# The first gate unit's first half between the two halves of keys and values, and the second half's keys from normalised operands

## The chip, the cores and the metric

The kernel runs on one core of one Trainium2 chip. The metric is device time of one execution in microseconds (us), the median of several runs; less is better. The engines are TensorE (PE in the profile; its weight loads are PEld), VectorE (DVE), ScalarE (ACT), GpSimd (POOL) and SyncE (SP), which issues most loads and stores. Each engine works through its own queue of instructions in order.

## What is computed

One layer of a decoder trunk on x of 2048 positions and 1024 channels, in float32:

```python
h = rms_norm(x, norm_g)
u = h @ w_in          # v_c, b_c, c_c, z_c, q, k, v, z_a, gate_logits
y_c = b_c * causal_depthwise_conv(c_c * v_c, conv_w) * silu(z_c)
y_a = y_c @ w_conv_out
q, k = rms_norm(q, q_norm_g), rms_norm(k, k_norm_g)      # per head
o = sliding_window_attention(q, k, v, sinks) * silu(z_a)  # window 128, blocks of 128
y_b = o @ w_attn_out
g_a, g_b = split(sigmoid(gate_logits + gate_b))
out = x + (g_a * y_a + g_b * y_b) @ w_out
```

There are 16 query heads and 4 key/value heads of 64. `norm_g` scales each channel, and the root of the mean square scales each position.

## The kernel before, in words

**Precision.** TensorE works on pairs: each operand is split into a rounded high part (a copy or cast on ACT) and the remainder, the low part (a subtraction on DVE). A product takes three passes: high by high, high by low, low by high.

**Tiles.** The 2048 positions are two tiles of 1024, each of two halves of 512. A projection of a tile is a "unit" of 256 columns. Most units (`sunit`, L645) use a seven-product scheme: the operands 1 to 7 are halves of the normalised input and sums of them, each in four pieces `oph_m_j` (`form`, L279/L310), and each product is 12 matmuls. The very first unit of a tile, the gate unit ("ga", 0, 0), is computed plainly (`qunit`, L767): for each half q of the positions and each half i of the 256 columns, 24 matmuls into one bank, `Qga`, from the operands `B_AT[p, q]`, that is 1 and 2 for the first half of the positions and 8 and 3 for the second.

**The opening.** Keys and values of the first tile come first, by token block (`kv_by_token`, L790): eight blocks of 128 positions, banks kv0 to kv7, 12 matmuls for each of four steps and pair of blocks. They read "plain" operands `opp_m_j`: x transposed times the channel gain, without the factor of the position, so that they can start before the mean squares are known; the positions' factor `rtok` is applied as the banks are read (`squares`, `values`). `plain_op` makes such an operand with one ACT and one DVE instruction. Meanwhile the rows of x (`x_load`, L819) are squared on ACT (`stats`, L824), `roots` makes `rtok` in small steps on DVE and ACT (`ms`, `hr_t`, `hr_r`; L293 to L306, L828), and `turned` turns it over on TensorE (`ptr`, L834) and copies it as `rb` to all partitions (L836). With `rb`, `norm_l` and `norm_r` scale x transposed in place for the first and second half, on DVE, and `form` splits it. The gate unit's bank goes through tanh on ACT (`fin_g`, L1430) and to HBM (SP).

**What sets the order.** The program is recorded step by step: `run` draws one "tick" at a time from a generator of matmuls, and after each tick records what tables have put there: `OPEN_AT` for the opening's operand work, `TURNED_AT`, `KV_PLACES`. Pieces of weights are split at one place per tick (`piece`, `force`). Each engine then takes its own instructions in the recorded order; an instruction that waits holds up all behind it on its engine. The loads are issued by SP: key/value weights and the first half of x transposed (`xt_load`, L1733), then in the order of `rows`, `first_w` and `xt_load` (L819, L1733, L443). Weights pass through two raw buffers (`raw`) that all units share.

**Attention.** Blocks of 64 query and key positions run through a chain of steps at the places of `STEPS_0`, among the units. The last product of a block is `po` (L1351) from `xh`, `yp` and `xl`, which POOL masks (L1334); `VALUES_LATER` puts single blocks one tick later.

Of the kernel before, what the change touches and what calls it, by code (L numbers as in the profile page):

```python
# [20 lines left out]
HB = H // P  # L21
# [5 lines left out]
UC = 256  # L27
# [9 lines left out]
WOVEN = 4  # L37
KV_BIG, W_FROM = 2, 10
W_LOADS = 0
KV_ORDER = 0  # L40
# [20 lines left out]
T0_SHIFT = 1  # L61
OPEN_AT = (2, 2, 2, 7, 7, 8, 5, 4, 5, 6, 4, 6, 5, 5, 7, 7, 9, 7, 7, 8, 7, 8, 8, 10, 12, 11, 14, 14, 14, 13, 17, 14, 14, 19, 18, 14, 16, 20, 20, 19, 20, 20, 18, 16, 19, 14, 20, 19, 22, 22, 23, 22, 23, 23, 8, 8, 14, 14, 26, 18, 22, 25, 27, 20, 26, 27, 21, 19, 23, 24, 18, 19, 19, 19, 28, 22, 28, 27)
KV_PLACES = (8, 11, 22, 26, 8, 11, 13, 40, 13, 31, 31, 30, 36, 36)
TURNED_AT = (7, 12)

# [18 lines left out]
SUM_WAIT = 5  # L84
VALUES_LATER = ((0, 10), (0, 30))
EARLY_LOADS = ((0, 29), (0, 30), (0, 31))
# [39 lines left out]
def block_kernel(  # L126
# [626 lines left out]
    def qunit(key, ops, fin):  # L753


        u = unit(key)
        nm = "_".join(str(i) for i in key)
        for q in range(2):
            for i in range(2):
                ps = bank(f"Q{nm}_{i}_{q}")  # L760
                for p in range(2):
                    force(u, (i, p))
                    hi, lo = ready[u][i, p]
                    for j in range(KP):
                        b = ops[B_AT[p, q]][j]
                        for k, (w, m) in enumerate(((hi, 0), (hi, 1), (lo, 0))):
                            nc.tensor.matmul(  # L767
                                ps, lhsT=w[:, j, :], rhs=b[:, m, :],
                                start=p == 0 and j == 0 and k == 0, stop=p == 1 and j == KP - 1 and k == 2)
                    if p:  # L770
                        fin(i, q, ps)
                        live[0] -= 2 * q
                    yield

    def kv_by_token(places, banks):


        for blocks, chunks, last in places:
            for c in chunks:
                hi, lo = ready[c // 4][c // 2 % 2]  # L780
                passes = [(b, k) for b in blocks for k in range(3)]
                if c == 0:
                    passes = [(b, k) for k in range(3) for b in blocks]
                for b, k in passes:
                    if b not in banks:
                        banks[b] = bank_of(b)
                    q, i = divmod(b, HB)
                    x = plain_ops[B_AT[c % 2, q]][c // 2]
                    m, w = ((0, hi), (0, lo), (1, hi))[k]
                    nc.tensor.matmul(  # L790
                        banks[b], lhsT=x[:, m, i * P : (i + 1) * P], rhs=w[c % 2],
                        start=c == 0 and k == 0, stop=c == KC - 1 and k == 2)
# [107 lines left out]

    def run(gen):
        while True:
            tick[0] += 1
# [28 lines left out]
    class KV:  # L932
# [5 lines left out]
        def squares(self, n):  # L938
# [5 lines left out]
            for k in range(2):  # L944
                b = 2 * n + k
                rooted[q]()
# [7 lines left out]
        def values(self, n):  # L954
            rooted[n // 2]()
            made = []
            for b in (2 * n, 2 * n + 1):
                v = slot([P, NKV, 2, HD], F32R, f"v0_{b}")
                src = self.banks[b][:, UC:].rearrange("p (j d) -> p j d", d=HD)
                r = rtok[:, b : b + 1]  # L960
                nc.scalar.activation(out=v[:, :, 0], in_=src, func=AF.Copy, scale=r)
# [462 lines left out]
    def fin_g(t, w, j):  # L1424
        def fin(i, q, val):
# [398 lines left out]
    put(OPEN_AT[7], lambda: plain_op(2, 1))
    put(OPEN_AT[8], lambda: plain_op(4, 1))
    put(OPEN_AT[9], lambda: plain_op(6, 1))
    put(OPEN_AT[10], lambda: plain_op(1, 1))
    put(OPEN_AT[11], lambda: plain_op(3, 1))
    put(OPEN_AT[12], lambda: plain_op(5, 1))
    put(OPEN_AT[13], lambda: plain_op(7, 1))  # L1830
# [11 lines left out]
    put(OPEN_AT[25], lambda: form(0, 1, 3, st))  # L1842
    put(OPEN_AT[26], lambda: norm_r(0, 0, st))
    put(OPEN_AT[27], lambda: norm_r(0, 2, st))
    put(OPEN_AT[28], lambda: norm_r(0, 4, st))
    put(OPEN_AT[29], lambda: norm_r(0, 6, st))
    put(OPEN_AT[30], lambda: form(0, 8, 0, st))
    put(OPEN_AT[31], lambda: form(0, 8, 1, st))
    put(OPEN_AT[32], lambda: form(0, 8, 2, st))
    put(OPEN_AT[33], lambda: form(0, 8, 3, st))  # L1850
    put(OPEN_AT[34], lambda: first_sum(0, st))
# [6 lines left out]
    put(OPEN_AT[41], lambda: form(0, 5, 3, st))  # L1858
    put(OPEN_AT[42], lambda: norm_r(0, 1, st))
    put(OPEN_AT[43], lambda: norm_r(0, 3, st))  # L1860
    put(OPEN_AT[44], lambda: norm_r(0, 5, st))
    put(OPEN_AT[45], lambda: norm_r(0, 7, st))
    put(OPEN_AT[46], lambda: second_sum(0, st))
# [22 lines left out]
    put(OPEN_AT[69], lambda: t4(3))  # L1886
    put(OPEN_AT[70], lambda: form(0, 3, 0, st))
    put(OPEN_AT[71], lambda: form(0, 3, 1, st))
    put(OPEN_AT[72], lambda: form(0, 3, 2, st))
    put(OPEN_AT[73], lambda: form(0, 3, 3, st))  # L1890
    put(OPEN_AT[74], lambda: form(0, 4, 0, st))
# [110 lines left out]
    for t in range(NT):  # L2002
# [193 lines left out]
```

## Time and profile before

| | us |
|---|---|
| median of 3 runs | 1894.96 (1894.78 to 1895.48) |
| the profiled execution's own time | 1895.86 |
| its span in the profile | 1894.2 |
| TensorE busy | 1887.7 |
| DVE busy | 1499.8 |
| ACT busy | 988.1 |
| POOL busy | 605.9 |

Rows of the profile give the line, the engine, the operation and "out<-in" by the program's names without buffer numbers. In a timeline the first two numbers are start and length in us; a bracket at the end gives the idle time before and what ended it. In the list of waits the numbers are the sum in us, the count and the longest. In groups they are the sum in us and the mean in ns, then the idle time before.

### The profile page before, as it was taken

The page shows a single profiled execution, that of the slowest core. Times are in us where ns is not written, and L with a number is a line of the kernel's source. Part 1 is how long each engine was busy: PE and PEld are TensorE (multiplying, and loading weights), DVE is VectorE, ACT ScalarE, POOL GpSimd, SP SyncE. Part 2 cuts the span into 40 slices and gives each one's busy share as a digit, 9 for nine tenths or more (in the row PEclk, how much of TensorE's full clock was granted, in tenths as well). Part 3 has the DMA queues.
Part 4 walks back from the last instruction along what each step waited for, and adds up shares of the span by engine and source line. Part 5 has one row for each costly group of instructions (what it writes and reads, how often), then busy time and mean ns, then how long its engine had stood idle before and what let it go on. Part 6 is the DMA issues. An engine that isn't in the chain of part 4 may idle for free.

```text
span 1894.2 us, 27255 instructions
## 1 busy us (share of the span) xinstructions
PE 1887.7 (100%) x8680; PEld 1572.9 (83%) x8680; DVE 1499.8 (79%) x2369; ACT 988.1 (52%) x1967; POOL 605.9 (32%) x847
## 2 busy tenths in 40 slices
PE   9999999999999999999999999999999999999999
PEld 7788888888888888888888888888888888888887
DVE  7988898887878767669799788887778867788654
ACT  7665455456666443434565455556666434444321
POOL 2074435336664000011372344445556000121000
PEclk9999999999999999999999999999999999999999
DMA  8286555558776957895584554567788867779653
GB/s 294 81 236 183 167 160 170 169 185 250 241 242 218 306 197 241 279 278 125 155 232 131 174 182 152 171 198 232 237 246 260 265 219 270 275 194 269 212 176 112
DMA packets 219727, 396.96 MB, mean 210 GB/s; under 512 B 29568, under 2 KB 104832, under 8 KB 210112
## 3 DMA queue, kind: packets, MB, share of 16 engines
q1 hardware_dynamic: 185312, 307.46, 50.0%
q0 software_dynamic: 30528, 78.94, 15.7%
q10 hardware_dynamic: 3744, 8.82, 1.4%
q8 instruction: 69, 1.13, 0.2%
q14 instruction: 74, 0.61, 0.1%
HBM read 266.90 MB, written 128.20 MB: 209 GB/s over the span
## 4 chain that ended last, share of the span: by engine, by line
PE 97%; DVE 1%; issue 1%; DMA 0%; ACT 0%; POOL 0%; DVEq 0%; ACTq 0%; POOLq 0%
PE Y L645 35%; PE Vcv L645 5%; PE Xcv L645 5%; PE ya L1492 4%; PE kv L790 2%; PE po L1351 2%; PE Vb L645 2%; PE Xgb L645 2%; PE Xq L645 2%; PE Vgb L645 2%; PE Vq L645 2%; PE Xb L645 2%; PE Xyb L645 2%; PE Vo L645 2%; PE Xo L645 2%; PE Vyb L645 2%
## 5 line engine op out<-in xcount | busy, mean ns | idle before, releaser
L1313 POOL DMA_DIRECT2D x<-fd x256 | 139.5, 552 | 114.0 <-DMA fd<-f 51.6
L1287 ACT ACTIVATE p<-s,st,rq 128x129 f32<-128x129 f32 x256 | 114.0, 456 | 32.3 <-DVE st L279 21.1
L1334 POOL TENSOR_SCALAR_AFFINE_SELECT xh<-xh 64x512 fp32r<-64x512 f32 x64 | 60.1, 940 | 156.6 <-DVE xl L279 96.1
L1306 POOL DMA_DIRECT2D fd<-f x64 | 36.9, 576 | 199.6 <-DVE f L279 174.0
L1575 POOL DMA_DIRECT2D mt<-tha x16 | 13.8, 861 | 254.9 <-DVE tha L279 241.3
L645 PE MATMUL Xcv<-oph,wcv_ah 128*128 128x512 f32 x256 | 78.9, 389 | 0.0
L1334 POOL TENSOR_SCALAR_AFFINE_SELECT xl<-xl 64x512 fp32r<-64x512 f32 x64 | 68.6, 1072 | 4.4
L1334 POOL TENSOR_SCALAR_AFFINE_SELECT yp<-xl 64x512 fp32r<-64x512 f32 x64 | 68.5, 1071 | 3.1
L1334 POOL TENSOR_SCALAR_AFFINE_SELECT yp<-yp 64x512 fp32r<-64x512 f32 x64 | 58.9, 920 | 4.2
L279 DVE TENSOR_TENSOR o<-po,o 64x256 f32<-64x256 f32 x128 | 53.5, 418 | 4.5 <-ACT o L1363 3.1
L279 DVE SCALAR_TENSOR_TENSOR y<-u,cols,y 128x512 f32<-128x512 f32 x64 | 53.6, 837 | 3.7 <-ACT y L1400 2.5
L645 PEld LDWEIGHTS Xcv<-oph,wcv_ah 128*128 128x128 f32 x256 | 47.8, 188 | 9.5
L472 ACT CAST wcv_sh<-wcv_raw 128x1024 fp32r<-128x1024 f32 x16 | 16.8, 1053 | 68.0 <-DVE wcv_raw L279 68.0
L279 DVE TENSOR_TENSOR p<-p,st 128x512 f32<-128x512 f32 x64 | 48.7, 762 | 3.4
L1091 POOL DMA_DIRECT2D q2d<-q_h x64 | 44.2, 691 | 21.9 <-issue 8.4
L1287 ACT ACTIVATION_READ_ACCUMULATOR p<-s,st,rq 128x1 f32 x256 | 51.2, 200 | 0.0
L645 PE MATMUL Xcv<-oph,wcv_al 128*128 128x512 f32 x128 | 49.9, 390 | 0.0
L1363 ACT COPY o<-po 64x256 f32<-64x256 f32 x128 | 47.0, 367 | 5.2 <-DMA wpd_yb<-wph_yb 2.3
L1262 PEld LDWEIGHTS s<-kq,q 128*128 128x128 f32 x256 | 46.1, 189 | 3.9
L2095 POOL DMA_DIRECT2D oc<-ocd x12 | 6.5, 543 | 133.8 <-ACT ophc L310 128.1
L1091 POOL DMA_DIRECT2D q2d<-q_l x64 | 44.1, 689 | 13.3 <-DMA q2d<-q_h 4.6
L279 DVE STREAM_TRANSPOSE f<-p 128x512 f32<-128x512 f32 x64 | 45.5, 711 | 2.8 <-DVE p L279 0.2
(723 smaller groups left out, 6411.6 us busy)
## 6 DMA issues: line engine op xcount, KB each, us to landing
gd<-th SPq DMA_DIRECT2D x64, 256.0 KB, 2.6
wcv_raw<-in_w_units SPq DMA_DIRECT2D x16, 1024.0 KB, 5.3
q<-q2d SPq DMA_DIRECT2D x64, 256.0 KB, 5.3
v<-vd SPq DMA_DIRECT2D x128, 128.0 KB, 3.6
fd<-f POOLq DMA_DIRECT2D x64, 256.0 KB, 4.3
x<-fd POOLq DMA_DIRECT2D x256, 64.0 KB, 3.6
th<-gd SPq DMA_DIRECT2D x48, 256.0 KB, 4.8
wga_raw<-in_w_units SPq DMA_DIRECT2D x8, 1024.0 KB, 5.3
```

Source lines behind the costliest of these rows:

```text
L279: r = f(*args, **kw)
L645: nc.tensor.matmul(ps, lhsT=w[:, j, :], rhs=b[:, m, cs], start=start and j == 0 and i == 0, stop=j == KP - 1 and i == 2, skip_group_check= ...
L790: nc.tensor.matmul(banks[b], lhsT=x[:, m, i * P : (i + 1) * P], rhs=w[c % 2], start=c == 0 and k == 0, stop=c == KC - 1 and k == 2)
L1091: nc.gpsimd.dma_start(q2d[t][j][half, q * 2 * HB : (q + 1) * 2 * HB, i, e, :], src[HALVES[e]].bitcast(F32).rearrange("p (b x) -> p b x", x ...
L1262: nc.tensor.matmul(sp[:, h, c, skip : 3 * HD], lhsT=q2[:, h, c, :], rhs=kq[:, 0, keys], start=c == 0, stop=False)
L1287: nc.scalar.activation(out=p[:, i, :], in_=sg[:, i, HD : 3 * HD + 1], func=AF.Exp, bias=st[:, 1, i : i + 1], scale=rv[:, i // 2, i % 2 : i ...
L1306: nc.gpsimd.dma_start(fd, f)
L1313: nc.gpsimd.dma_start(x[QUADS[k]], src[k])
L1334: nc.gpsimd.affine_select(out=d4, in_=s4, pattern=[[0, 2], [-32 * sg, 2], [0, G], [-sg, 32]], compare_op=ALU.is_gt if prev else ALU.is_ge, ...
L1351: nc.tensor.matmul(po[:, cs], lhsT=v2[:, kind + h, :], rhs=xx[:, :, h * HD : (h + 1) * HD], start=n == h == 0, stop=n == 2 and h == 1)
L1363: nc.scalar.copy(ov, pov[oth, :, e])
L1492: nc.tensor.matmul(ps, lhsT=w[:, j, cs], rhs=o[:, m, :], start=n == 0 and i == 0, stop=n == KC - 1 and i == 2)
```

## The change

Five things change, four of them in the opening.

1. The gate unit's first half of positions (48 matmuls, `run(first_unit, 4)`) is recorded between the two halves of keys and values instead of after them. It reads the plain operands, so its two banks lack the positions' factor: `fin_g` multiplies them by `rb` on DVE and puts the tanh several ticks later. These two banks come from another pool (`mbank`).
2. The second half of keys and values reads operands made from the normalised second half (`second_half`: for each chunk `norm_r`, then `form`, all eight chunks at tick 11), not plain ones. The eight plain operands of that half go, and the same `oph_8_j` and `oph_3_j` now serve keys, values and the gate unit's second half. Their banks are read without the factor.
3. Loads: the first gate unit's weights go ahead of all rows of x, and the second rows of x ahead of the second half of x transposed. Pieces of weights may be split from tick 1.
4. The tables of places are set anew.
5. `VALUES_LATER` gains a block: tile 0, r = 28, that is `po0_3_4`.

```diff
-KV_BIG, W_FROM = 2, 10
-W_LOADS = 0
+KV_BIG, W_FROM = 2, 1
+W_LOADS = 3
+SECOND_AT = 11
...
-TURNED_AT = (7, 12)
+TURNED_AT = (9, 11)
...
-VALUES_LATER = ((0, 10), (0, 30))
+VALUES_LATER = ((0, 10), (0, 28), (0, 30))
...
-                ps = bank(f"Q{nm}_{i}_{q}")
+                ps = bank(f"Q{nm}_{i}_{q}") if q else mbank(f"Q{nm}_{i}_{q}").rearrange("p b q -> p (b q)")
...
-                        b = ops[B_AT[p, q]][j]
+                        b = ops[q][B_AT[p, q]][j]
...
-                    x = plain_ops[B_AT[c % 2, q]][c // 2]
+                    x = (st["ops"] if q else plain_ops)[B_AT[c % 2, q]][c // 2]
...
-                    out=nat[:, k], in_=self.banks[b][:, 0:UC], func=AF.Copy, scale=rtok[:, b : b + 1])
+                    out=nat[:, k], in_=self.banks[b][:, 0:UC], func=AF.Copy,
+                    scale=1.0 if q else rtok[:, b : b + 1])
...
+            elif (t, w, j, q) == (0, 0, 0, 0):
+                mul(th, val, state[0]["rb"][0])
+                put(18 + 2 * i, lambda: act(th))
...
     first_w(3)
     rows(0)
-    first_w(2)
+    rows(1)
     for c in range(KC):
         xt_load(c, 1)
-    first_w(1)
-    rows(1)
...
+    def second_half(j):
+        for e in range(2):
+            norm_r(0, 2 * j + e, st)
+            form(0, B_AT[e, 1], j, st)
+
...
-    put(OPEN_AT[6], lambda: plain_op(0, 1))
...
+    for j in range(KP):
+        put(SECOND_AT, lambda j=j: second_half(j))
...
     run(kv_by_token(first, kv.banks))
     zero_prev()
+    first_unit = qunit(("ga", 0, 0), (plain_ops, st["ops"]), fin_g(0, 0, 0))
+    run(first_unit, 4)
     run(kv_by_token([((4 + 2 * n, 5 + 2 * n), (2 * k, 2 * k + 1), n == 1) for n, k in (
...
-            run((qunit if t == n == 0 else sunit)(key, ops, fin))
+            run(first_unit if t == n == 0 else sunit(key, ops, fin))
```

**TensorE, at the end of the first half of keys and values.** kv0 to kv3 are the first half's banks, kv4 and kv5 the second's; `opp` are plain operands. Before:

```order
L790 MATMUL kv3_265<-wkv3_1h_223,opp_2_3_231 128x512
L790 MATMUL kv4_462<-wkv0h_183,opp_8_0_350 128x512
L790 MATMUL kv5_464<-wkv0h_183,opp_8_0_350 128x512
L790 MATMUL kv4_462<-wkv0l_184,opp_8_0_350 128x512
L790 MATMUL kv5_464<-wkv0l_184,opp_8_0_350 128x512
```

Now, with the first factor's transposes (`ptr0_0`) twelve matmuls into the gate unit:

```order
L791 MATMUL kv3_267<-wkv3_1h_223,opp_2_3_231 128x512
L768 MATMUL Qga_0_0_0_0_397<-opp_1_0_186,wga_0_0_p0h_279 128x512 x2
L768 MATMUL Qga_0_0_0_0_397<-opp_1_0_186,wga_0_0_p0l_280 128x512
L768 MATMUL Qga_0_0_0_0_397<-opp_1_1_198,wga_0_0_p0h_279 128x512 x2
L768 MATMUL Qga_0_0_0_0_397<-opp_1_1_198,wga_0_0_p0l_280 128x512
L768 MATMUL Qga_0_0_0_0_397<-opp_1_2_212,wga_0_0_p0h_279 128x512 x2
L768 MATMUL Qga_0_0_0_0_397<-opp_1_2_212,wga_0_0_p0l_280 128x512
L768 MATMUL Qga_0_0_0_0_397<-opp_1_3_226,wga_0_0_p0h_279 128x512 x2
L768 MATMUL Qga_0_0_0_0_397<-opp_1_3_226,wga_0_0_p0l_280 128x512
L835 MATMUL ptr0_0_410<-ident_129,rtok_148 128x128 x4
```

And 36 matmuls into it the second factor's transposes, twelve matmuls later the first of kv4 from the normalised operand (kv4 and kv5 share a tile, so both read kv4):

```order
L768 MATMUL Qga_0_0_1_0_463<-opp_1_3_226,wga_0_0_p1l_298 128x512
L835 MATMUL ptr0_1_476<-ident_129,rtok_148 128x128 x4
L768 MATMUL Qga_0_0_1_0_463<-opp_2_0_191,wga_0_0_p1h_297 128x512 x2
L768 MATMUL Qga_0_0_1_0_463<-opp_2_0_191,wga_0_0_p1l_298 128x512
L768 MATMUL Qga_0_0_1_0_463<-opp_2_1_203,wga_0_0_p1h_297 128x512 x2
L768 MATMUL Qga_0_0_1_0_463<-opp_2_1_203,wga_0_0_p1l_298 128x512
L768 MATMUL Qga_0_0_1_0_463<-opp_2_2_217,wga_0_0_p1h_297 128x512 x2
L768 MATMUL Qga_0_0_1_0_463<-opp_2_2_217,wga_0_0_p1l_298 128x512
L768 MATMUL Qga_0_0_1_0_463<-opp_2_3_231,wga_0_0_p1h_297 128x512 x2
L768 MATMUL Qga_0_0_1_0_463<-opp_2_3_231,wga_0_0_p1l_298 128x512
L791 MATMUL kv4_545<-wkv0h_183,oph0_8_0_484 128x512 x2
```

The 48 gate matmuls moved in front of the second half; each factor's transposes moved from among key/value matmuls to among gate matmuls.

**DVE, the second half's operands.** Before, one instruction each behind the first `rtok`, the low parts of the plain operands:

```order
L828 COPY rtok_148<-hr0_0_r_299 128x4
L279 SCALAR_TENSOR_TENSOR opp_8_1_332<-xt2_158,cols_120,opp_8_1_332 128x512
L279 SCALAR_TENSOR_TENSOR opp_3_0_335<-xt1_155,cols_120,opp_3_0_335 128x512
L279 SCALAR_TENSOR_TENSOR opp_8_0_350<-xt0_121,cols_120,opp_8_0_350 128x512
L279 SCALAR_TENSOR_TENSOR opp_8_2_353<-xt4_163,cols_120,opp_8_2_353 128x512
```

Now, behind the second `rtok`, a norm with the second factor (`rb0_1`) and a low part in turn; ahead of them stand the multiply at the gate bank and the value remainders of two blocks:

```order
L280 TENSOR_TENSOR th0_0_0_0_442<-Qga_0_0_0_0_397,rb0_0_415 128x512
L306 SCALAR_TENSOR_TENSOR hr0_4_t_425<-hr0_4_t_425,ms0_4_423 128x4
L280 SCALAR_TENSOR_TENSOR v0_0_451<-kv0_262,rtok_148,v0_0_451 128x4x64
L307 SCALAR_TENSOR_TENSOR hr0_4_r_424<-hr0_4_t_425,hr0_4_r_424 128x4
L280 SCALAR_TENSOR_TENSOR v0_1_453<-kv0_262,rtok_148,v0_1_453 128x4x64
L829 COPY rtok_148<-hr0_4_r_424 128x4
L280 SCALAR_TENSOR_TENSOR xt0_121<-xt0_121,cols_120,rb0_1_481 128x512
L280 TENSOR_TENSOR oph0_8_0_484<-xt0_121,oph0_8_0_484 128x512
L280 SCALAR_TENSOR_TENSOR xt1_155<-xt1_155,cols_120,rb0_1_481 128x512
L280 TENSOR_TENSOR oph0_3_0_488<-xt1_155,oph0_3_0_488 128x512
L280 SCALAR_TENSOR_TENSOR xt2_158<-xt2_158,cols_120,rb0_1_481 128x512
L280 TENSOR_TENSOR oph0_8_1_492<-xt2_158,oph0_8_1_492 128x512
```

The pairs go on for all eight chunks; on ACT the eight casts (`oph0_8_0` and so on) stand in the same order behind the copy of `rb0_1`.

**ACT, ahead of the first query unit's copy of Xq into Y.** Before:

```order
L310 CAST oph0_6_3_826<-xt6_170 128x512
L1430 ACTIVATE th0_0_1_1_844<-Qga_0_0_1_1_807,hbias_145 128x512
L472 CAST wq_0_0_th_847<-wq_0_0_raw_277 128x1024
L665 COPY Y_147<-Xq_0_0_853 128x512
L674 COPY s5q_0_0_883<-Vq_0_0_870 128x512
```

Now:

```order
L473 CAST wq_0_0_sh_760<-wq_0_0_raw_277 128x1024
L950 ACTIVATE k0_2_n_774<-kv4_545 128x256 x2
L953 ACTIVATE ksq0_2_773<-k0_2_n_774 128x512
L311 CAST oph0_6_0_791<-xt0_121 128x512
L311 CAST oph0_6_1_794<-xt2_158 128x512
L311 CAST oph0_6_2_797<-xt4_163 128x512
L311 CAST oph0_6_3_800<-xt6_170 128x512
L1435 ACTIVATE th0_0_1_1_816<-Qga_0_0_1_1_778,hbias_145 128x512
L473 CAST wq_0_0_th_819<-wq_0_0_raw_277 128x1024
L966 ACTIVATE v0_6_827<-kv6_636 128x4x64
L966 ACTIVATE v0_7_829<-kv7_638 128x4x64
L666 COPY Y_147<-Xq_0_0_837 128x512
```

The values of the last two blocks (`v0_6`, `v0_7`) now stand ahead of that copy, and the last casts of operand 6 closer to it.

More of the change, by code (lines that the diff above doesn't have):

```diff
@@ L61 @@
 T0_SHIFT = 1
-OPEN_AT = (2, 2, 2, 7, 7, 8, 5, 4, 5, 6, 4, 6, 5, 5, 7, 7, 9, 7, 7, 8, 7, 8, 8, 10, 12, 11, 14, 14, 14, 13, 17, 14, 14, 19, 18, 14, 16, 20, 20, 19, 20, 20, 18, 16, 19, 14, 20, 19, 22, 22, 23, 22, 23, 23, 8, 8, 14, 14, 26, 18, 22, 25, 27, 20, 26, 27, 21, 19, 23, 24, 18, 19, 19, 19, 28, 22, 28, 27)
-KV_PLACES = (8, 11, 22, 26, 8, 11, 13, 40, 13, 31, 31, 30, 36, 36)
-TURNED_AT = (7, 12)
+OPEN_AT = (3, 3, 3, 8, 9, 9, 5, 4, 5, 6, 4, 6, 5, 5, 9, 9, 9, 9, 14, 14, 14, 14, 13, 13, 13, 13, 11, 11, 11, 11, 11, 11, 11, 11, 16, 16, 17, 17, 17, 17, 18, 18, 11, 11, 11, 11, 19, 19, 20, 20, 23, 23, 23, 23, 15, 15, 15, 15, 24, 24, 24, 24, 25, 25, 26, 26, 22, 22, 22, 22, 11, 11, 11, 11, 27, 27, 28, 28)
+KV_PLACES = (10, 12, 22, 26, 10, 12, 17, 24, 15, 31, 31, 30, 36, 36)
+TURNED_AT = (9, 11)
 K_ROOT = True
@@ L899, in put, with run @@
         at.setdefault(max(n, tick[0] + 1), []).append(f)
-    def run(gen):
-        while True:
+    def run(gen, n=None):
+        while n is None or n > 0:
+            n = n and n - 1
             tick[0] += 1
@@ L945, in squares @@
                 b = 2 * n + k
-                rooted[q]()
+                if q == 0:
+                    rooted[q]()
                 nc.scalar.activation(
-                    out=nat[:, k], in_=self.banks[b][:, 0:UC], func=AF.Copy, scale=rtok[:, b : b + 1])
+                    out=nat[:, k], in_=self.banks[b][:, 0:UC], func=AF.Copy,
+                    scale=1.0 if q else rtok[:, b : b + 1])
             nc.scalar.activation(out=sq, in_=nat.rearrange("p k c -> p (k c)"), func=AF.Square)
@@ L954, in values @@
         def values(self, n):
-            rooted[n // 2]()
+            if n < 2:
+                rooted[0]()
             made = []
@@ L959, in values @@
                 src = self.banks[b][:, UC:].rearrange("p (j d) -> p j d", d=HD)
-                r = rtok[:, b : b + 1]
+                r = rtok[:, b : b + 1] if b < HB else 1.0
                 nc.scalar.activation(out=v[:, :, 0], in_=src, func=AF.Copy, scale=r)
@@ L1820, in block_kernel @@
     put(OPEN_AT[4], lambda: stats(1, 2))
-    put(OPEN_AT[5], lambda: roots(1))
     put(TURNED_AT[1], lambda: turned(1))
-    put(OPEN_AT[6], lambda: plain_op(0, 1))
[L1824 to L1830, printed above, removed]
     put(OPEN_AT[14], lambda: norm_l(0, 0, st))
@@ L1834, in block_kernel @@
     put(OPEN_AT[17], lambda: norm_l(0, 6, st))
+    put(OPEN_AT[5], lambda: roots(1))
+    for j in range(KP):
+        put(SECOND_AT, lambda j=j: second_half(j))
     put(OPEN_AT[18], lambda: norm_l(0, 1, st))
@@ L1842, in block_kernel @@
     put(OPEN_AT[25], lambda: form(0, 1, 3, st))
[L1843 to L1850, printed above, removed]
     put(OPEN_AT[34], lambda: first_sum(0, st))
@@ L1858, in block_kernel @@
     put(OPEN_AT[41], lambda: form(0, 5, 3, st))
[L1859 to L1862, printed above, removed]
     put(OPEN_AT[46], lambda: second_sum(0, st))
@@ L1886, in block_kernel @@
     put(OPEN_AT[69], lambda: t4(3))
[L1887 to L1890, printed above, removed]
     put(OPEN_AT[74], lambda: form(0, 4, 0, st))
@@ L1907, in bank_of @@
             return bank(f"kv{b}")
-        if b in (4, 5):
+        if b in (6, 7):
             return mbank(f"kv{b}").rearrange("p b q -> p (b q)")
```

## The prediction

> **What bounds the kernel now.** I read the page first: busy times and the chain that ended last.
>
> ```profile
> PE 1887.7 (100%) x8680; PEld 1572.9 (83%) x8680; DVE 1499.8 (79%) x2369; ACT 988.1 (52%) x1967; POOL 605.9 (32%) x847
> PE 97%; DVE 1%; issue 1%; DMA 0%; ACT 0%; POOL 0%; DVEq 0%; ACTq 0%; POOLq 0%
> ```
>
> TensorE is busy 1887.7 of 1894.2 us and is 97% of the chain. The change neither adds nor drops a matmul, so it can win only TensorE's idle time and lose only by making TensorE wait. Next, all the waits of TensorE:
>
> ```profile
> PE Y L1738 <- DVE zero L200: 1.1, 1, 1.1
> PE Qga L767 <- DVE oph L279: 1.0, 2, 0.8
> PE po L1351 <- POOL xl L1334: 0.6, 1, 0.6
> PE kv L790 <- ACT opp L1747: 0.2, 1, 0.2
> PE po L1351 <- POOL yp L1334: 0.2, 1, 0.2
> ```
>
> The first and the fourth lie ahead of the changed code. What can be won is Qga and po. Their full price, with the restart, is read from TensorE's timeline (start, length):
>
> ```profile
> 1.12 3.78 PE L1738 MATMUL Y<-zero 128*128 128x512 f32 x8 [1.12 <-DVE zero L200]
> 25.40 0.60 PE L834 MATMUL ptr<-ident,rtok 128*128 128x128 f32 x4
> 25.75 0.48 PE L790 MATMUL kv<-wkv_1h,opp 128*128 128x512 f32 x1
> 28.63 0.63 PE L790 MATMUL kv<-wkv0h,opp 128*128 128x512 f32 x2
> 51.12 0.63 PE L767 MATMUL Qga<-oph,wga_p0h 128*128 128x512 f32 x2
> 62.04 0.62 PE L767 MATMUL Qga<-oph,wga_p0h 128*128 128x512 f32 x2
> 67.75 0.50 PE L767 MATMUL Qga<-oph,wga_p0h 128*128 128x512 f32 x1 [0.77 <-DVE oph L279]
> 74.50 0.62 PE L645 MATMUL Xq<-oph,wq_ah 128*128 128x512 f32 x2
> 85.38 0.62 PE L645 MATMUL Y<-oph,wq_th 128*128 128x512 f32 x2
> 576.46 0.40 PE L1351 MATMUL po<-xh,v 128*128 128x256 f32 x2
> 577.17 0.63 PE L645 MATMUL Vz<-oph,wz_th 128*128 128x512 f32 x2
> 588.90 0.40 PE L1351 MATMUL po<-xh,v 128*128 128x256 f32 x2
> 590.98 0.63 PE L645 MATMUL Y<-oph,wz_sh 128*128 128x512 f32 x2
> ```
>
> The gate unit's first 48 matmuls take 62.04 - 51.12 = 10.92 us (0.2275 each), its second 48 take 12.46: 1.54 lost. Four transposes hold TensorE 0.35 us (25.40 to 25.75), so the 96 key/value matmuls from 28.63 to 51.12 take 22.49 - 0.35 = 22.14 (0.2306 each). The stalled po block takes 2.08 us, an unstalled one 0.71: 1.37 lost. Together 2.9 us, or 0.15%, is the most that can be won; about 0.2% is what a measurement of this kernel tells from no change.
>
> **The change part by part.**
>
> *Loads.* The rows below (ACT and DVE, opening) serve this part and the next.
>
> ```profile
> 16.36 0.62 ACT L310 CAST wkv_0h<-wkv_raw 128x512 fp32r<-128x512 f32 x1 [0.32 <-DMA wkv_raw<-in_wkv]
> 21.49 1.06 ACT L824 ACTIVATE x<-x 128x1024 f32<-128x1024 f32 x1 [1.28 <-DMA x<-in_x]
> 28.82 0.56 ACT L836 COPY rb<-ptr 128x512 f32<-128x512 f32 x1
> 29.28 1.06 ACT L824 ACTIVATE x<-x 128x1024 f32<-128x1024 f32 x1
> 29.72 4.06 DVE L279 SCALAR_TENSOR_TENSOR xt<-xt,cols,rb 128x512 f32<-128x512 f32 x6
> 33.70 0.16 DVE L293 TENSOR_SCALAR ms<-ss 128x4 f32<-128x4 f32 x1
> 33.89 0.21 ACT L300 ACTIVATE hr_t<-ms 128x4 f32<-128x4 f32 x1 [0.33 <-DVE ms L293]
> 34.00 1.65 ACT L310 CAST oph<-xt 128x512 fp32r<-128x512 f32 x3
> 37.81 0.48 DVE L279 SCALAR_TENSOR_TENSOR v<-kv,rtok,v 128x256 fp32r<-128x256 f32 x1 [1.07 <-ACT v L961]
> 38.67 0.16 DVE L828 COPY rtok<-hr_r 128x4 f32<-128x4 f32 x1
> ```
>
> The last key/value weight landed at 16.36, the fourth 512 KB row block at 21.49: 1.28 us each. Now 1 MB of gate weights (2.56) goes ahead of them, and the eighth block lands near 16.36 + 2.56 + 8 x 1.28 = 29.2, the second half of x transposed (2 MB, 5.1) near 34.3. Both are ahead of their first use below: nothing. The gate load takes over the raw buffer of the first key/value weights, so SP waits for their last reader with the blocks of x behind it; the transfers issued before still run until 16.36 and cover that. Were the blocks 2 us later, the second factor would come that much later too.
>
> *The second factor.* The first key/value half loses its transposes and ends at 28.63 - 0.35 = 28.28. The first factor's transposes stand after 12 gate matmuls, at 31.01; ACT copies it from 31.64 to 32.20. Two row squares stand behind that copy (1.06 each, to 34.3), and on DVE four norms: six took 4.06 and one is 0.74, so 0.66 apart, 32.23 to 34.96. So `ms` starts at 34.88 and the root at 35.07 (0.16 and a hand-over of 0.03, as at 33.70 and 33.89). From 33.89 the factor took 4.94 us to the end of `rtok`, 38.83; three casts (1.55) in that stretch have moved away, so it ends at 35.07 + 3.39 = 38.46. TensorE is at its second transposes at 31.01 + 0.35 + 24 x 0.2275 = 36.82 and waits until 38.5: 1.7 us. Behind them in its queue stand twelve gate matmuls and all of the second key/value half. Then 0.60, a hand-over and the copy: the first norm of the second half starts at 39.73.
>
> *Eight operands, one after the other.* DVE's new order is norm, low part, norm, low part; each low part needs ACT's cast of the norm just ahead of it, so nothing overlaps. Three groups of the first 100 us give the lengths (mean ns after the bar), and a run of three low parts their spacing:
>
> ```profile
> L279 DVE TENSOR_TENSOR oph<-xt,oph 128x512 fp32r<-128x512 f32 x28 | 18.2, 678 | 0.5 <-ACT oph L310 0.3
> L279 DVE SCALAR_TENSOR_TENSOR xt<-xt,cols,rb 128x512 f32<-128x512 f32 x16 | 11.5, 741 | 0.0
> L310 ACT CAST oph<-xt 128x512 fp32r<-128x512 f32 x28 | 16.2, 617 | 8.5 <-DVE xt L279 7.9 <-DVE oph L279 0.4
> 60.41 1.88 DVE L279 TENSOR_TENSOR oph<-xt,oph 128x512 fp32r<-128x512 f32 x3
> ```
>
> One chunk is 0.74 + 0.03 + 0.62 + 0.03 + 0.60 (three of 0.68 end in 1.88, so the next starts 0.60 later) = 2.02 us; TensorE uses one up in 6 x 0.2306 = 1.38. The first is whole at 41.83, the eighth at 41.83 + 7 x 2.02 = 55.97; four matmuls then remain (0.92): 56.94 with the hand-over. Without waits it would be 36.82 + 0.35 + 2.73 + 11.07 = 50.97. First delay: 6.0 us, the 1.7 within it. The following 48 + 48 matmuls (21.99) find their operands ready, so the query unit starts at 78.93 instead of 74.50: +4.43, the old 1.54 being gone. No alternating chain stands in the trace; the chunk's bounds are 1.27 (0.66 + 0.60 of DVE alone) and 2.12 (full lengths with both hand-overs). I take 2.02, as a wait for ACT holds DVE (the 1.07 at 37.81).
>
> [...]
>
> *What comes due next.* The eight plain operands (one ACT and one DVE instruction each) are gone; DVE gains two multiplies by the factor (the two tanh and their stores behind them on SP have no reader near) and is now late elsewhere. From 55.89 it has this ahead of operand 7's first low part: 41 of half width (0.60), 4 of full width, 4 norms (0.66), 3 pairs of value remainders, and the key root.
>
> ```profile
> 42.49 0.88 DVE L279 SCALAR_TENSOR_TENSOR v<-kv,rtok,v 128x256 fp32r<-128x256 f32 x2
> 47.06 0.17 DVE L293 TENSOR_SCALAR k_ms<-kss 128x16 f32<-128x16 f32 x1
> 47.89 0.74 DVE L279 SCALAR_TENSOR_TENSOR xt<-xt,cols,rb 128x512 f32<-128x512 f32 x1
> 56.80 1.21 DVE L279 TENSOR_TENSOR wq_al<-wq_raw,wq_ah 128x1024 fp32r<-128x1024 f32 x1
> 57.94 0.68 DVE L279 TENSOR_TENSOR xt<-xt 128x512 f32<-128x512 f32 x1
> ```
>
> 24.6 + 4 x 1.14 + 2.7 + 3 x 0.8 + 1.0 (0.83 and two small steps) + an estimated 0.5 of waits = 35.8: it starts at 91.7 and ends at 92.4. TensorE wants it at its second matmul of that product, 78.93 + (85.38 - 74.50) + 0.23 = 90.04. Second delay: 2.4 us, between 0 (DVE 2.4 earlier) and 3.5. ACT's copy of Xq into Y, which product 6 needs, now stands behind the values of two more blocks and behind casts that wait for the late DVE; its lateness lies within the same 2.4. Afterwards the operands are there and DVE's order is the old one.
>
> *Values one step later.* The block's po moves behind the next product (about 2.7 us); its remainder was 0.65 late. -1.37, between -1.37 and 0.
>
> *Sum:* +4.43 + 2.4 - 1.37 = +5.5 us. On the profiled execution's own 1895.86 us that is 1901.4; the median of the runs shown is 0.9 lower, and 1894.96 + 5.5 = 1900.5.
>
> **The rivals.**
>
> *The cast is hidden (not slower).* If DVE could run a norm ahead of ACT, chunks would cost 1.27, below TensorE's 1.38, and only the 1.7 remains at the first place; DVE comes 5 us earlier, so the second delay is gone: +1.7 - 1.54 - 1.37 = -1.2, 1893.8. It decides at 1.38 us a chunk. Against it: the order, in which each low part stands directly behind its own norm. Chance 0.07.
>
> *No second delay.* If the query unit's operands keep up, +4.43 - 1.37 = +3.1: 1898.0. For it: DVE's 35.8 is a sum of 60 spacings, and 4% less takes more than half of the delay. Chance 0.16.
>
> *A slower TensorE.* The opening's first eight matmuls took 3.78 us, 0.47 each, twice the later pace; if gaps of 0.6 us in every 2.02 bring that pace back, a chunk takes 2.8 and the stretch 6.4 more: 1906.9. Against it: 0.50 then the old pace after the 0.77 gap at 67.75. Chance 0.05. [...]
>
> **How the numbers follow.** Forecast 0.64; the rivals 0.07, 0.16, 0.05; 0.08 is left for what I have not seen. The predicted time is the forecast's, 1900.5. Its own bounds are about 1.5 us either way; the range reaches down past the rival without a second delay, to 1897.6, and up by 2.9 (second delay at its upper end, chunks at 2.12, waits that I missed) to 1903.4. Slower by over 0.2% starts at 1898.75: nearly all of the forecast, a third of the second rival, all of the third, part of the rest: 0.75. Within 0.2%: 0.23, the first rival among it. Faster: 0.02.
>
> **What would show it.** Right: in the stretch from 40 to 57 us kv waits for DVE eight times or so, DVE's busy share falls there while its norms and low parts alternate about 2 us apart; one wait of the second transposes for `rtok`; Xq first at about 79, a wait in its product 6 or 7; no po wait near 590. Wrong: kv waits summing to under 3 us, Xq starting before 77, or new waits of TensorE after 130 us.

## The result, and the profile after

The changed kernel is slower: 1905.54 us against 1894.68 (medians of six runs each), ratio 1.0059 (95% interval 1.0049 to 1.0070), +10.9 us. Forecast were +5.5 and at most 1903.4. The direction was right, the size was half of what came.

The profiled execution took 1905.32 us with a span of 1903.6. First the page's busy times and the list of all waits of TensorE:

```profile
PE 1892.2 (99%) x8680; PEld 1572.4 (83%) x8680; DVE 1496.7 (79%) x2363; ACT 984.8 (52%) x1959; POOL 603.0 (32%) x847
PE Y L646 <- DVE Vq L280: 2.9, 1, 2.9
PE ptr L835 <- DVE rtok L829: 1.6, 1, 1.6
PE Vq L646 <- ACT th L1435: 1.4, 1, 1.4
...
```

The two rows left out lie in the first 6 us. TensorE is busy 4.5 us longer with the same 8680 matmuls, so some of the loss hides in "busy". No wait is later than 100 us. Next, TensorE's timeline at the landmarks (start, length):

```profile
38.28 0.62 PE L835 MATMUL ptr<-ident,rtok 128*128 128x128 f32 x4 [1.57 <-DVE rtok L829]
78.96 0.62 PE L646 MATMUL Xq<-oph,wq_ah 128*128 128x512 f32 x2
83.23 0.73 PE L646 MATMUL Vq<-oph,wq_sh 128*128 128x512 f32 x2 [1.39 <-ACT th L1435]
94.59 1.19 PE L646 MATMUL Y<-oph,wq_th 128*128 128x512 f32 x2 [2.91 <-DVE Vq L280]
98.93 0.62 PE L646 MATMUL Vq<-oph,wq_th 128*128 128x512 f32 x2
603.19 0.63 PE L646 MATMUL Xz<-oph,wz_ah 128*128 128x512 f32 x2
```

The same rows of before started at 74.50 (Xq), 77.22 (Vq), 85.38 (Y), 88.10 (Vq again) and 593.75 (Xz):

```profile
77.22 0.62 PE L645 MATMUL Vq<-oph,wq_sh 128*128 128x512 f32 x2
88.10 0.62 PE L645 MATMUL Vq<-oph,wq_th 128*128 128x512 f32 x2
593.75 0.62 PE L645 MATMUL Xz<-oph,wz_ah 128*128 128x512 f32 x2
```

So the shift is +4.46 where the query unit starts, +6.01 at its fifth product, +9.21 at its seventh, +10.83 at its third, and +9.44 behind the moved block of values. Between 94.59 and 98.93 twelve matmuls took 4.34 us instead of 2.72: the first two took 1.19. Busy times by window, cut where the clock changed (start:end, length, busy time of PE, PEld, DVE, ACT, POOL, then the granted clock), show why:

```profile
91.01:94.42 3.41, 0.68 (x3) 0.21 (x2) 3.41 (x8) 3.38 (x7) 2.47 (x4) 1.00 0.81 308
94.42:97.84 3.42, 3.25 (x8) 2.60 (x9) 3.42 (x6) 2.24 (x5) 0.00 (x0) 0.50 0.47 158
97.84:101.25 3.41, 3.41 (x17) 2.81 (x16) 3.34 (x7) 0.00 (x0) 0.00 (x0) 1.00 0.00 0
```

After a window in which TensorE was busy 0.68 of 3.41 us, the clock was 0.50 for 3.41 us.

DVE's timeline shows the chain and what the seventh product waited for:

```profile
39.56 0.75 DVE L280 SCALAR_TENSOR_TENSOR xt<-xt,cols,rb 128x512 f32<-128x512 f32 x1 [1.43 <-ACT rb L837]
41.00 0.69 DVE L280 TENSOR_TENSOR oph<-xt,oph 128x512 fp32r<-128x512 f32 x1 [0.69 <-ACT oph L311]
41.61 0.75 DVE L280 SCALAR_TENSOR_TENSOR xt<-xt,cols,rb 128x512 f32<-128x512 f32 x1
...
55.28 0.69 DVE L280 TENSOR_TENSOR oph<-xt,oph 128x512 fp32r<-128x512 f32 x1 [0.68 <-ACT oph L311]
...
91.35 2.49 DVE L280 TENSOR_TENSOR oph<-xt,oph 128x512 fp32r<-128x512 f32 x4
93.75 0.69 DVE L280 TENSOR_TENSOR Vq<-s5q,Y 128x512 f32<-128x512 f32 x1
```

The add starts only when the four low parts of operand 7 are through. ACT's timeline shows what the fifth product waited for:

```profile
78.25 1.05 ACT L473 CAST wq_sh<-wq_raw 128x1024 fp32r<-128x1024 f32 x1 [3.49 <-DVE wq_raw L280]
80.43 2.16 ACT L311 CAST oph<-xt 128x512 fp32r<-128x512 f32 x4
82.50 0.68 ACT L1435 ACTIVATE th<-Qga,hbias 128x512 f32<-128x512 f32 x1
```

The serial chain is as forecast: first norm 39.56, chunks 2.04 apart, the last low part ends at 55.97. What it cost TensorE is not in its own list of waits: between 39 and 57 us that list has nothing behind the transposes. PE's records there carry modelled ends, and the waits stand at its weight loads:

```profile
PEld kv L791 <- ACT oph L311: 3.7, 7, 0.6
PEld kv L791 <- DVE oph L280: 3.0, 7, 0.4
```

The fifth product's bank was the gate unit's. Its last tanh stood in ACT's queue behind a weight cast that waited 3.49 us for DVE, and behind operand 6's casts. The seventh product writes Y, which DVE's add `Vq<-s5q,Y` has to read first.

### The profile page after: what moved, and what is told of

It is laid out like the page before. It is cut to its first block, busy times and chain, and to the rows that moved or that the text cites. A ratio compares the mean times of both kernels' runs of the same rounds, so it can differ in the third digit from the quotient of the medians.

```text
span 1903.6 us, 27215 instructions
## 1 busy us (share of the span) xinstructions
PE 1892.2 (99%) x8680; PEld 1572.4 (83%) x8680; DVE 1496.7 (79%) x2363; ACT 984.8 (52%) x1959; POOL 603.0 (32%) x847
## 4 chain that ended last, share of the span: by engine, by line
PE 95%; DVE 3%; ACT 1%; DMA 1%; issue 0%; SPq 0%; DVEq 0%; ACTq 0%
PE Y L646 35%; PE Vcv L646 5%; PE Xcv L646 5%; PE ya L1500 4%; PE po L1356 2%; PE Vb L646 2%; PE Xgb L646 2%; PE Vz L646 2%; PE Vgb L646 2%; PE Xb L646 2%; PE Xz L646 2%; PE Xyb L646 2%; PE Vyb L646 2%; PE Vza L646 2%; PE Xza L646 2%; PE Xo L646 2%
```

## The experiments

**The theory.** From 55.89 to 94.44 us DVE hardly idles: it is busy 38.13 of 38.55 us. TensorE reaches the seventh product when DVE has reached the add, whatever it waits for on the way; behind that wait, 2.91 us, comes the half clock (0.50 for 3.41 us). **Rivals:** each wait is a cost of its own (the chain, the bank, the low parts); or the halved clock comes from the chain's many gaps.

**The moved block of values alone.**

```diff
-VALUES_LATER = ((0, 10), (0, 30))
+VALUES_LATER = ((0, 10), (0, 28), (0, 30))
```

> The kernel before with the one later block of values (tile 0, r = 28) and nothing else. Theory: the stall of 1.4 us near 589 is in every execution and goes, so 1.4 us less than before, about 1893.3. Rival: the mask on POOL is late in the profiled execution alone, or the next product only takes over the wait: no difference, 1894.7.

Measured: 1894.09 against 1894.27, ratio 1.0001 (0.9992 to 1.0009). The stall near 589 is gone from this trace, yet no gain is shown; the interval, -1.5 to +1.7 us, just reaches the 1.4 us that were expected. The list of waits has another wait in place of it, at 448 us. A cast on ACT had waited 5.74 us for a transfer there, and DVE's next instruction reads that cast. The traces of the kernel before and of the changed one have none there:

```profile
PE Y L645 <- DVE th L279: 1.4, 1, 1.4
```

The times alone do not decide, but the theory said that the stall is in every execution. The run with stalls, below, has the old place of the block in a second trace, and the stall is all but gone there. So the theory fell: waits of this size come and go between executions.

**The chain with one norm ahead.**

```diff
     def second_half(j):
+        if j == 0:
+            norm_r(0, 0, st)
         for e in range(2):
-            norm_r(0, 2 * j + e, st)
+            if 2 * j + e + 1 < KC:
+                norm_r(0, 2 * j + e + 1, st)
             form(0, B_AT[e, 1], j, st)
```

> The changed kernel with one norm recorded ahead of each split (norm, norm, low, norm, low ...), so that ACT's cast lies beside the next norm. Both theories: chunks 1.3 us apart instead of 2.04, the key/value waits of 40 to 57 us all but gone, Xq starts at 74.6 instead of 78.96. Theory (the second delay is DVE's backlog): DVE, which had idled 5.5 us in the chain, is only that much earlier at the add Vq<-s5q,Y, near 88.5 instead of 93.75; TensorE is 4.4 us earlier at the place that needs it, so a wait of about 3 us stays at the seventh product and the halved clock behind it too: 5.5 us less than the changed kernel, about 1900. Rival (the second delay only follows from TensorE's gaps and the bank held by the gate unit): the waits at the fifth and seventh product and the halved clock go as well, 10 us less, about 1895.5.

Measured: 1900.49, ratio to before 1.0034 (1.0021 to 1.0048), 5.0 us less than the changed kernel. First DVE's groups from 39 to 50 us:

```profile
L280 DVE SCALAR_TENSOR_TENSOR xt<-xt,cols,rb 128x512 f32<-128x512 f32 x8 | 5.9, 745 | 1.4 <-ACT rb L837 1.4
L280 DVE TENSOR_TENSOR oph<-xt,oph 128x512 fp32r<-128x512 f32 x8 | 5.5, 685 | 0.1
```

The low parts wait 0.1 us (the last column) instead of 5.5. TensorE's query unit and its seventh product:

```profile
74.14 0.62 PE L646 MATMUL Xq<-oph,wq_ah 128*128 128x512 f32 x2
88.40 0.70 PE L646 MATMUL Y<-oph,wq_th 128*128 128x512 f32 x2 [2.90 <-DVE Vq L280]
```

The query unit starts 4.8 us earlier, and the wait of 2.9 us stands where it was. The bank's wait of 1.39 us at the fifth product is gone, as the rival had it. (The profiled execution, 1902.63, also lost time near 453 us: a wait of 2.08 us, and the twelve matmuls behind it took 4.36 us instead of 2.72.) The theory holds for the seventh product: curing the chain brings TensorE sooner to the same late DVE. The chain's gaps are gone and TensorE still slowed behind that wait (the low pass at 89.70 takes 0.63 us, others 0.39; the execution's mean clock is 0.998), so they did not cause it.

**The bank freed sooner.** Operand 6's four splits (entries 50 to 53 of the table) and a pair of key squares go behind the last tanh.

```diff
-OPEN_AT[50:54] = 23, 23, 23, 23
+OPEN_AT[50:54] = 24, 24, 24, 24
-KV_PLACES = (10, 12, 22, 26, 10, 12, 17, 24, 15, 31, 31, 30, 36, 36)
+KV_PLACES = (10, 12, 24, 26, 10, 12, 17, 24, 15, 31, 31, 30, 36, 36)
```

> The changed kernel with operand 6's splits and one pair of key squares recorded behind the last tanh of the first gate unit, so that its bank is free when the fifth product wants it. Both theories: the wait of 1.4 us at the fifth product goes. Theory (DVE's work sets when the seventh product starts): the seventh product still starts at 94.6 and its wait grows by as much: 0 us, 1905.5. Rival (the bank's wait is a cost of its own, added to the others): 1.5 us less, 1904.0.

Measured: 1907.99, ratio 1.0070 (1.0056 to 1.0084). TensorE's rows of the sixth and the seventh product:

```profile
85.32 0.73 PE L646 MATMUL Y<-oph,wq_sh 128*128 128x512 f32 x2 [0.66 <-ACT Y L666]
94.69 1.19 PE L646 MATMUL Y<-oph,wq_th 128*128 128x512 f32 x2 [3.30 <-DVE Vq L280]
```

The fifth product no longer waits, and the seventh starts 0.1 us from where it did. Two windows behind it, with the clock as the third number from the end:

```profile
94.06:97.47 3.41, 2.78 (x7) 2.23 (x8) 3.41 (x6) 2.44 (x5) 0.00 (x0) 0.50 0.20 56
97.47:100.89 3.42, 3.42 (x10) 2.65 (x9) 2.50 (x5) 0.00 (x0) 0.00 (x0) 0.50 0.00 0
```

In place of the bank's wait, 0.66 us came at the sixth product and 0.39 more at the seventh, so it was no cost of its own. In this trace the clock was 0.50 for 6.83 us instead of 3.41, and the third product starts 1.0 us later than in the changed kernel; the profiled execution, 1906.36, is 1.0 us longer too. The median is 2.4 us longer, and what the other 1.4 us are stays open.

**The add ahead of the low parts, twice.** First, operand 7's splits move whole behind the add; then only their low parts, with the casts left in place.

```diff
-OPEN_AT[62:66] = 25, 25, 26, 26
+OPEN_AT[62:66] = 27, 27, 27, 27
```

```diff
+        if (t, m) == (0, 7):
+            o = new_op("h0", m, j, st["ops"])
+            src = st["raw"][2 * j, 1]
+            nc.scalar.copy(o[:, 0], src)
+            lows7.append((o, src))
+            return
...
+    put(27, late_lows)
```

> The changed kernel with the four splits of operand 7 recorded behind the add Vq<-s5q,Y, on which the seventh product's writes into Y wait. Theory (that product waits for the add, which stands behind four low parts): the add ends at 92.0 instead of 94.4, the product starts there with a wait of 0.4 us instead of 2.9, and the clock is not halved after so short a wait: 2.4 + 1.7 = 4.1 us less, about 1901.4, and the trace shows a clock of 1.0 throughout. Rival 1 (the low parts of operand 7 bound the product, as the prediction had it): TensorE waits for them inside the product instead, 0.7 us less, 1904.8. Rival 2 (the halved clock follows from the gaps of 40 to 57 us or from the opening, not from this wait): 2.4 us less, 1903.1, with the clock still halved.

> The changed kernel with only the four low parts of operand 7 recorded behind the add Vq<-s5q,Y; their casts on ACT stay where they were, which the earlier try did not do. Theory (the seventh product waits for the add, and the add stands behind four low parts): the add ends at 92.0 instead of 94.4, TensorE idles 0.4 us instead of 2.9 and its clock is not halved: 2.4 + 1.7 = 4.1 us less, about 1901.4. Rival (DVE's backlog bounds the product itself, whatever its order): TensorE waits inside the product for the low parts, 0.7 us less, 1904.8.

Measured: 1905.66 (ratio 1.0060, 1.0047 to 1.0074) and 1903.95 (1.0047, 1.0033 to 1.0061). The first was no test of the theory: the casts now stood behind a copy that waited 4.25 us for DVE, and TensorE waited for them instead. First ACT's row of the copy:

```profile
91.20 0.71 ACT L950 ACTIVATE k_n<-kv 128x256 f32<-128x256 f32 x2 [4.25 <-DVE v L280]
```

That copy pushed the four casts to 93.42, and TensorE's row shows whom it waits for:

```profile
94.09 0.49 PE L646 MATMUL Y<-oph,wq_th 128*128 128x512 f32 x1 [2.32 <-ACT oph L311]
```

The wait is 2.32 us for a cast, in place of 2.91 for the add. The second, whose opening ran 1.9 us late in this trace (last section), shows in TensorE's rows:

```profile
93.95 1.09 PE L646 MATMUL Y<-oph,wq_th 128*128 128x512 f32 x2 [0.39 <-DVE Vq L280]
101.79 1.39 PE L646 MATMUL Y<-oph,wq_d 128*128 128x512 f32 x5 [1.30 <-DVE q_t L280]
```

The wait fell from 2.91 to 0.39 (its query unit starts at 80.84 against 78.96, so the product starts at 93.95 - 1.88 = 92.07 on the changed kernel's clock) and no halved clock shows (the execution's mean is 1.0, the changed kernel's 0.999), as expected. But 1.30 us came back at the fourth product, which waits for DVE's next sum of Y. DVE's arrears had moved, not gone: 1.6 us less in the medians instead of 4.1.

**The second part undone.** Keys and values of the second half read plain operands again, with the factor at their banks.

```diff
-                    x = (st["ops"] if q else plain_ops)[B_AT[c % 2, q]][c // 2]
+                    x = plain_ops[B_AT[c % 2, q]][c // 2]
...
-SECOND_AT = 11
+SECOND_AT = 13
...
+    for c in range(KC):
+        put(10, lambda c=c: plain_op(c, 1))
```

> The changed kernel with its second part undone: the second half of keys and values reads plain operands again (eight plain operands more, the factor applied at its banks), and the normalised operands of that half follow at tick 13 for the gate unit's second half alone. Theory (the time is set by how much work DVE has up to the add Vq<-s5q,Y, since TensorE waits there anyway): the key/value waits go and Xq starts near 74.5, but DVE has 5.9 us more work, of which some 2.5 fit into its idle time before 39.6; the add comes some 3 us later, near 97, and the seventh product waits over 8 us: 1906 to 1909. Rival (the serial chain costs TensorE directly, and only the chain): 4.5 to 6 us less than the changed kernel, about 1900.

Measured: 1907.40, ratio 1.0070 (1.0056 to 1.0084). TensorE's first matmuls of the second half, its query unit, and its fifth and seventh product:

```profile
43.28 0.70 PE L791 MATMUL kv<-wkv0h,opp 128*128 128x512 f32 x2 [1.99 <-DVE v L280]
...
78.56 0.73 PE L646 MATMUL Xq<-oph,wq_ah 128*128 128x512 f32 x2 [0.48 <-ACT th L1433]
...
87.23 1.22 PE L646 MATMUL Vq<-oph,wq_sh 128*128 128x512 f32 x2 [5.66 <-ACT th L1433]
98.54 0.70 PE L646 MATMUL Y<-oph,wq_th 128*128 128x512 f32 x2 [0.49 <-DVE Vq L280]
```

The query unit starts at 78.56, not near 74.5 as expected: TensorE waited 1.99 us for DVE's value remainders, which read a bank, and its clock was 0.50 for 3.41 us behind that wait (the execution's mean is 0.997). The large wait has moved to the fifth product. DVE's add in the same trace:

```profile
97.70 0.69 DVE L280 TENSOR_TENSOR Vq<-s5q,Y 128x512 f32<-128x512 f32 x1
```

The add comes 3.95 us later, and TensorE's seventh product too. The tanh for which the fifth product waits stood on ACT behind a weight cast that itself waited 3.57 us for DVE; the sum is DVE's. So the time follows DVE's work, which is the theory. What the chain alone costs TensorE is not shown here, since other waits took its place; the run with the norm ahead shows that.

**Stalls put into the kernel before.** In ten units of the second tile the add is repeated, with the same result each time (`STALL` gives 5 to 12 repeats, more from unit to unit):

```diff
         add(vb, s5, Y)
+        for _ in range(STALL.get(key, 0)):
+            nc.vector.tensor_tensor(out=vb, in0=s5, in1=Y, op=ALU.add)
```

> The kernel before with its add vb = s5 + Y repeated 5 to 12 times on DVE in ten units of the second tile, so that TensorE idles once in each, between about 0.3 and 5 us; the opening is untouched. [...] Rival (the halving in the changed kernel came from its many short gaps before): the clock stays at 1.0 throughout. Beside it: whether the stall at the block of values near 589 is there in a second profile of this schedule.

Measured: one execution, 1949.79 us with all the stalls. Windows around two of the ten, idle for 3.33 us (1012.28 to 1015.61) and for 3.25 us (1105.01 to 1108.26):

```profile
1010.88:1014.29 3.41, 1.40 (x7) 0.82 (x5) 3.24 (x7) 0.63 (x1) 0.00 (x0) 1.00 0.96 346
1014.29:1017.71 3.42, 2.10 (x5) 1.71 (x6) 3.39 (x5) 1.49 (x3) 0.00 (x0) 0.50 0.52 158
1017.71:1021.12 3.41, 3.41 (x9) 2.64 (x9) 1.96 (x4) 0.69 (x2) 0.00 (x0) 0.50 0.04 10
...
1103.04:1106.45 3.41, 1.97 (x9) 1.31 (x7) 3.24 (x6) 1.95 (x7) 0.00 (x0) 1.00 0.66 187
1106.45:1109.87 3.42, 1.61 (x7) 1.35 (x8) 3.35 (x6) 0.00 (x0) 0.99 (x1) 1.00 0.10 31
1109.87:1113.28 3.41, 3.41 (x17) 2.82 (x16) 3.27 (x5) 0.00 (x0) 3.23 (x4) 1.00 0.00 0
```

The first idles 2.01 us within one window, and the clock is 0.50 in the next two, to 1021.12; the second idles 1.44 us in one and 1.81 in the next, and the clock is 1.00 in all three. So a single wait, here of 3.33 us, can be followed by half clock with none of the opening's gaps; the other, of 3.25 us, was not. The same trace has the old block of values:

```profile
588.08 0.40 PE L1354 MATMUL po<-xh,v 128*128 128x256 f32 x2
589.05 0.63 PE L646 MATMUL Y<-oph,wz_sh 128*128 128x512 f32 x2
```

Here it takes 0.97 us, not 2.08: a stall of 0.26 instead of 1.37.

**Starting DVE sooner, step by step.** Four kernels build on the run with the norm ahead. First the last two row squares and the second root move from step 9 to 8, and the second factor's transposes from 11 to 10. Then the first key squares and values also move from 10 to 9. Then operand 7's low parts go behind the add as well. Last, two splits of operand 4 move from 28 to 29, behind the sum of Y.

```diff
-OPEN_AT[4:6] = 9, 9
+OPEN_AT[4:6] = 8, 8
-TURNED_AT = (9, 11)
+TURNED_AT = (9, 10)
...
-KV_PLACES = (10, 12, 22, 26, 10, 12, 17, 24, 15, 31, 31, 30, 36, 36)
+KV_PLACES = (9, 12, 22, 26, 9, 12, 17, 24, 15, 31, 31, 30, 36, 36)
...
-OPEN_AT[76:78] = 28, 28
+OPEN_AT[76:78] = 29, 29
```

> The changed kernel with three repairs: one norm ahead of each split; the last two row squares and the second root recorded ahead of the copy of the first factor; the second factor's transposes after 24 gate matmuls instead of 36. Theory (all that was lost comes from DVE starting late on the second half and idling in the chain): the second factor is ready near 33.5 instead of 38.1, DVE's norms start near 35 instead of 39.6 and do not idle, so DVE is 4.5 + 5.5 = 10 us earlier at the add, near 84; TensorE, without any wait up to there, is at its seventh product at 83.8. No wait over 0.5 us, no halved clock, Xq at about 73: 1.5 us less than before, about 1892.8. Rival (the halves of x transposed or the row blocks land too late for that, or POOL and ACT become the bound): the second factor stays near 38, as before or up to 1.6 us more than the run with the norm ahead would give less, 1897 to 1900.

> The run with three repairs, and the first pair of key squares and values recorded one step earlier, ahead of the second factor's copy, since in that run DVE stood 2.24 us at the values' low part with the norms behind it. Theory (DVE's backlog at the add sets the seventh product): the first norm comes at 37.2 instead of 38.9, the add 1.6 us earlier, the wait of 2.9 us at the seventh product falls to 1.3 and the clock is no longer halved: 1.6 + 1.5 = 3.1 us less than that run, about 1895.3. Rival (the wait there does not follow DVE's start): 2.9 us and the halved clock stay, 1898.4.

> The same, and the four low parts of operand 7 behind the add, as in the run of the casts. Theory: the add comes another 2.4 us earlier, so no wait is left at the fifth, seventh or fourth product, and the clock stays whole; what remains against the kernel before is that its two waits of the gate unit (1.54 us in its profile, 0.9 in the second one) are gone too: 1 to 1.5 us less than before, about 1893.2, and faster than both kernels. Rival (the wait only moves on, as in the run of the casts, where 1.3 us of it came back at the fourth product for the sum of Y and s5): about 1894.5 to 1895, the same as before.

> The run with all repairs, and the last two splits of operand 4 recorded one step later, behind the sum of Y and s5 for which the fourth product waited 1.2 us there. Theory (that wait is again only DVE's order): the sum comes 1.2 us earlier, the wait goes, no other takes its place in the first 130 us: 1.2 us less than that run and than before, about 1893.9. Rival (the fourth product now waits for operand 4's late pieces instead): no gain, 1895.1.

| | us | ratio to before (95%) | wait at the seventh product |
|---|---|---|---|
| norm ahead | 1900.49 | 1.0034 (1.0021 to 1.0048) | 2.90 |
| and the factor sooner | 1898.36 | 1.0021 (1.0012 to 1.0030) | 2.90 |
| and the first values sooner | 1896.15 | 1.0009 (1.0000 to 1.0018) | 1.68 |
| and the low parts behind the add | 1895.07 | 0.9999 (0.9990 to 1.0008) | none |
| and operand 4 behind the sum | 1893.93 | 0.9998 (0.9989 to 1.0007) | none |

Each row has its own runs of the kernel before beside it (medians 1894.27 to 1895.11), so the ratios compare better than the times. The second row missed its number by 5.6 us. The factor did come sooner, but two instructions ahead of the norms on DVE waited for ACT, as its rows show:

```profile
34.44 0.16 DVE L829 COPY rtok<-hr_r 128x4 f32<-128x4 f32 x1
...
38.09 0.88 DVE L280 SCALAR_TENSOR_TENSOR v<-kv,rtok,v 128x256 fp32r<-128x256 f32 x2 [2.24 <-ACT v L966]
38.88 1.41 DVE L280 SCALAR_TENSOR_TENSOR xt<-xt,cols,rb 128x512 f32<-128x512 f32 x2
```

The third row moved them, and the wait fell by 1.2 us (1.6 expected), with the mean clock at 1.0. That trace is of the fastest of eleven runs (1894.47 to 1900.11), so the others may have waited longer. In the fourth row, 1.16 us came back at the fourth product, which is what its rival said; the last one took that wait away too. TensorE's list there, whose first two rows are the first 6 us:

```profile
PE Y L1754 <- DVE zero L201: 1.1, 1, 1.1
PE kv L791 <- ACT opp L1763: 0.7, 1, 0.7
...
```

The rest is 0.3 and less. The ratio hardly moved with that last step (0.9999 to 0.9998), so no gain of it is shown in the times, and neighbouring rows' intervals overlap; it is the way from the first row to the last two that is clear of noise. So the change's loss is DVE's order and start, as far as these runs can tell. With both repaired the new arrangement equals the old one within 0.1%; its median is 0.8 us lower, which the interval does not tell from no difference. No version here is shown to beat the kernel before.

## What the prediction had right, and the step that failed

- **Loads, the second factor:** right. The second transposes waited 1.57 (forecast 1.7).
- **Eight operands, one after the other:** right: 2.04 us a chunk (2.02), last low part at 55.97 (55.97), query unit at 78.96 (78.93). First delay +4.46 against +4.43. That close an agreement is partly luck: the first norm came 0.17 us earlier than forecast, and the seven chunks behind the first took 0.14 more. Putting a norm ahead gave it all back, 4.8 us at that place.
- **What comes due next, "Second delay: 2.4 us":** the step that failed. The sum for DVE was right, since operand 7's first low part ended at 92.03 (91.35 + 0.68; forecast 92.4). Wrong was what TensorE needs there. "TensorE wants it at its second matmul of that product" looked at the operand alone; the product also overwrites Y, and its last reader, the add, is queued behind all four low parts. TensorE waits for 94.44, not 92.03. Without a second delay the product would start at 85.38 + 4.46 = 89.84, so the delay is 4.75 up to its start at 94.59, and another 1.62 by the halved clock up to the third product (10.83 - 9.21): 6.4 in all, where the prediction had 2.4 and at most 3.5. About 2.4 of the missing 4.0 us lie between the first low part and the end of the add (94.44 - 92.03), and 1.6 are the halved clock, which this term had at nothing. That ACT's "lateness lies within the same 2.4" holds in kind: the bank's 1.39 was not added, as the run that freed it shows.
- **"Slower TensorE", a rival at 0.05:** named in the wrong place. Gaps of some 0.66 us in every 2.04 left the clock at 1.00 from 40 to 57 us. Behind one gap of 2.91 it was 0.50 for 3.41 us.
- **"Values one step later. -1.37":** a second failed term. The two profiles differ there by 1.4 (10.83 to 9.44), but the change alone showed no gain, and the old block stalls 0.26 in another execution. The profiled execution of before, 1895.86, lies above all six runs compared here (1894.08 to 1895.48). A wait seen once was taken for one that is always there.
- **The sum:** 4.46 + 6.4 + 0 = 10.9, and the medians differ by 10.86. That these agree so closely is partly luck: the terms come from one pair of traces, and the measured ratio leaves 9.3 to 13.3 us.

## What to carry to other kernels

For a product that writes into a bank, list the last readers of the bank as well as its operands, and find each in its engine's queue. When one engine hands out work without a pause, removing single waits of the consumer only moves the wait (the bank's 1.39 us came back as 0.66 and 0.39); sum that engine's work and idle time up to the last hand-over. Take a stall that may depend on transfers from two executions before pricing its removal.

## What the runs showed of the hardware

Behind TensorE's waits the clock was 0.50 for 3.41 us in the changed kernel (from 94.42), for 6.83 us in the run that freed the bank (from 94.06), and from 1014.29 to 1021.12 in the run with stalls. Of windows of 3.41 us at whole clock in the run with stalls, one with 2.01 us of idle time was followed by 0.50, those with 1.44, 1.71 and 1.81 us were not; in the first run of the add one with 1.62 us, in two pieces, was. So these runs show no length of idle time that parts the two. A wait of 3.25 us was followed by whole clock, and one of 2.91 cost 1.62 us beyond itself in the changed kernel. In the run that freed the bank TensorE idled only 0.63 us in a window at 0.50 (94.06 to 97.47), and the next was at 0.50 too.

TensorE's pace in the opening also differs between traces. In the changed kernel's trace the first four key/value matmuls start at 5.29 and the ninth at 7.53, so the eight took 0.33 and then 0.23 us each. In the second run of the add, the first eight key/value matmuls still took 0.43 to 0.49 each, and everything behind them came 1.9 us later than in the changed kernel (0.5 of it since they started at 5.79 instead of 5.29):

```profile
5.79 2.15 PE L791 MATMUL kv<-wkv0h,opp 128*128 128x512 f32 x4 [0.89 <-ACT opp L1763]
7.74 1.91 PE L791 MATMUL kv<-wkv0l,opp 128*128 128x512 f32 x4
```

What brings the faster pace is not shown. What the waits near 450 us depend on (1.45 us with the block of values alone, 2.08 with the norm ahead), which come in some traces and not in others, stays open.
